# A heads' softmax turned by DMA instead of TensorE, with the value product two pairs later

## The chip, the cores and the metric

The kernel runs on one core of a Trainium2 chip. The metric is the device time of one execution in microseconds (us). The time before the change is 2466.49 us, the median of three runs (2465.38 to 2469.66). The core has TensorE (PE in the profile; its weight loads are listed as PEld), VectorE (DVE), ScalarE (ACT), GpSimd (POOL), and SyncE (SP), whose queue issues most DMA transfers.

## The reference: what is computed

One layer of an encoder on 256 tokens of width 2048, all in float32. Four residual blocks follow one another, each with a layer norm: a SwiGLU network, a mixer of two attention branches, a cross attention to 256 memory tokens, and a second SwiGLU network. The change touches branch A of the mixer: 16 heads of width 64 that look at 64-token chunks, with a clipped relative bias. With 256 tokens and eight previous chunks in view, it is causal by chunk.

```python
def chunked_relbias_attention(q, k, v, rel_bias):
    ...
    scores = jnp.einsum('bcqhd,bckhd->bchqk', qc, kb).astype(jnp.float32) / math.sqrt(d)
    ...
    scores = jnp.where(valid[None, :, None, None, :], scores + bias[None, None], NEG_INF)
    p = jax.nn.softmax(scores, axis=-1).astype(v.dtype)
    o = jnp.einsum('bchqk,bckhd->bcqhd', p, vb)
    return o.reshape(b, s, h * d)

def hybrid_mixer(u, w_in, gate_bias, rel_bias, q_a_norm, w_q_b, kv_a_norm, w_kv_b,
                 w_o_a, w_o_b, w_out, cos, sin):
    ...
    y_a = chunked_relbias_attention(qa.reshape(shp), ka.reshape(shp), va.reshape(shp), rel_bias) @ w_o_a
    y_b = mla_attention(q_lat, kv_lat, q_a_norm, w_q_b, kv_a_norm, w_kv_b, cos, sin) @ w_o_b
    ...
    return (g_a * y_a + g_b * y_b) @ w_out
```

## The kernel before

Weights come in as float32 tiles of 128 x 2048 (1 MB). Each is loaded by a DMA from SP's queue into one of three `raw` buffers, cast by ACT into a `hi` part (fp32r), and the rest is computed by DVE as a `lo` part; there are two buffers each for `hi` and `lo` (`halves`, L245 to L254). Matmuls run over `hi` and `lo` separately (`mm_wide`, L263 and L265): 16 `hi` matmuls of 512 columns, which hold both parts of the activation, and 16 `lo` matmuls of 256.

The program is a list of items, recorded with `add` in the order of the computation, each with the weight tiles that it consumes. `run` walks through it. Before each item it records the loads of the coming weight tiles, as far as two `hi`/`lo` buffers allow, and then the item itself. In the A stage this means that after the first projection of a pair (q) the load of the next pair's first tile is recorded, and after the second (k) that of its second tile. A scheduler then writes out a fixed order for each engine: among the instructions whose inputs are ready by its own reckoning, the one recorded first comes first, with some groups moved ahead by a priority. The softmax has such a priority of 100 instructions. `issue_after` adds an order between two instructions of the same engine without a wait on a result.

Branch A works in eight pairs of heads. For pair i the items are the projections of pair i+1 (`a_proj`, two weight tiles), the turn of pair i−1 (`a_trans`), the scores of pair i with bias and softmax (`a_scores`), and the value product of pair i−1 (`a_out`). Both heads of a pair share the 128 partitions: 64 rows each for the scores, 64 columns each for the value product. The softmax of one head is a 128 x 384 tile: 128 queries by 128 keys, and 128 queries by 256 keys. The value product needs it with keys on partitions. So `a_trans` calls `transpose_p`, which transposes three 128 x 128 blocks of each head on PE (L824) into PSUM and copies them out with ACT (L830). The value product is `pv` (L1027 and L1028). Softmax results and turned tiles are in the `w2` group of working buffers, of which there are six.

During pairs 0 and 1 the latent vectors of branch B are turned as well (`lat_turn`, L927). At the end of A come the rope projections (`rope_items`, weights `w_qr`), whose swap of rows is done by eight small DMAs on SP (L942), and the first heads of B (`b_proj`, weights `w_v` and `w_nope`, and `b_scores`). Two `w2` buffers hold the rope tables then, which POOL loads (L525).

The feed-forward networks do not turn their hidden layer on PE. Their `hidden` copies the float32 words into two planes of 16-bit halves (ACT, L714), sends them through a transposing DMA on SP (L719), and joins the halves again (ACT, L725).

Of the kernel before, what the change touches and what calls it, by code (L numbers as in the profile page):

```python
# [12 lines left out]
U16 = mybir.dt.uint16  # L13
# [5 lines left out]
P = 128  # L19
# [75 lines left out]
class Kernel:  # L95
    def __init__(self, ctx, tc, t, out):
        self.tc, self.nc, self.t, self.out = tc, tc.nc, t, out

        def pool(name, bufs=1, **kw):
            return ctx.enter_context(tc.tile_pool(name=name, bufs=bufs, **kw))  # L100

        self.const = pool("const")
        self.wraw = pool("wraw", 3)
        self.whi = pool("whi", UNITS)
        self.wlo = pool("wlo", UNITS)
        self.blocks = pool("blocks")
        self.res = pool("res")
        self.work = pool("work", 4)
        self.small = pool("small", 4)
        self.ps_mm = pool("ps_mm", 4, space=PSUM)  # L110
        self.ps_at = pool("ps_at", 4, space=PSUM)
        self.items = []
        self.uid = 0
        self.chain = None
        self.cut = False


# [54 lines left out]
    def run(self):  # L172
        queue = [w if isinstance(w, (tuple, Sums)) else (w, None) for _, ws, _, _ in self.items for w in ws]
        ready, nxt, live = [], 0, 0

        def slots(w):
            return 0 if isinstance(w, tuple) and w[1] else 1

        raws, sums = {}, {}

        def fetch(i):
            if i not in raws:
                ap = queue[i].ap if isinstance(queue[i], Sums) else queue[i][0]
                raws[i] = self.raw_tile()
                self.last_load = self.nc.sync.dma_start(raws[i][:, :ap.shape[1]], ap)
            return raws[i]

        def form_sums(i):
            if i < len(queue) and isinstance(queue[i], Sums) and i not in sums:
                raw, home = fetch(i), queue[i].stage  # L190
                sums[i] = self.weight_sums(raw, queue[i].m, self.block(home, (P, 2048)) if home else self.raw_tile())

        def load(i):
            w = queue[i]
            raw = fetch(i)
            form_sums(i)
            if isinstance(w, Sums):
# [12 lines left out]

        def ahead(need, held):
            if nxt < need:
                return True
            n = sum(not early(w) for w in queue[need:nxt])
            return (nxt < need + 5 and (early(queue[nxt]) or n < 2)
                    and held + live + slots(queue[nxt]) <= UNITS)

        done, highs = 0, []
        for fn, ws, held, prio in self.items:
            need = done + len(ws)  # L220
            while nxt < len(queue) and ahead(need, held):
# [471 lines left out]
    def hidden(self, ps, j, g, n, hid, qs):  # L693

        nc = self.nc
        s, u = {}, {}

        def words(v):
            return v.bitcast(U16)

        def product():
            for tt in range(2):
                if qs:
                    up, s[tt] = (qs["add"][tt, a] for a in range(2))
                    nc.vector.tensor_tensor(s[tt], s[tt], ps[tt, 1][:, :n * P], ALU.add)
                    nc.vector.tensor_tensor(up, up, ps[tt, 0][:, :n * P], ALU.add)
                    nc.scalar.activation(s[tt], s[tt], AF.Silu)
                    nc.vector.scalar_tensor_tensor(s[tt], up, 0.5, s[tt], ALU.mult, ALU.mult)
                    u[tt] = up
                else:  # L710
                    s[tt], u[tt] = (self.w2()[:, :n * P] for _ in range(2))
                    nc.scalar.activation(s[tt], ps[tt, 1][:, :n * P], AF.Silu)
                    nc.vector.scalar_tensor_tensor(s[tt], ps[tt, 0][:, :n * P], 0.5, s[tt], ALU.mult, ALU.mult)
                nc.scalar.copy(words(u[tt]).rearrange("p (k c) -> p k c", k=2),  # L714
                               words(s[tt]).rearrange("p (c k) -> p k c", k=2))

        def send():
            for tt in range(2):
                nc.sync.dma_start_transpose(words(s[tt]).rearrange("p (b q) -> p b q", q=P), words(u[tt]))  # L719

        def turn():
            hid.blocks += self.act([f"H{g}"]).blocks
            for tt in range(2):
                with self.tc.issue_after(self.next_hi.ins):
                    nc.scalar.copy(words(u[tt]).rearrange("p (c k) -> p k c", k=2),  # L725
                                   words(s[tt]).rearrange("p (k c) -> p k c", k=2))
# [79 lines left out]
    def softmax(self, s, spans, src=None, scale=1.0):  # L806
        nc = self.nc
        src = s if src is None else src
        n = len(spans)
        m, r = self.sm("sm_m", 2), self.sm("sm_r", 2)  # L810
        for i, (a, b) in enumerate(spans):
            nc.vector.tensor_reduce(m[:, i:i + 1], src[:, a:b], AX.X, ALU.max)
        nc.vector.tensor_scalar(m, m, -scale, None, ALU.mult)
        for i, (a, b) in enumerate(spans):
            nc.scalar.activation(s[:, a:b], src[:, a:b], AF.Exp, bias=m[:, i:i + 1], scale=scale,
                                 accum_out=r[:, i:i + 1])
        nc.vector.reciprocal(r, r)
        for i, (a, b) in enumerate(spans):
            nc.vector.tensor_scalar(s[:, a:b], s[:, a:b], r[:, i:i + 1], None, ALU.mult)

    def transpose_p(self, s, cols, halves=False):
        ps = self.at_tile()
# [11 lines left out]
    def mixer(self, xT, st, steps):  # L834
# [131 lines left out]
        qk, sc, pt = {}, {}, {}  # L966
        oA = {}

        def a_proj(i, side=()):
            def one(k):  # L970
                def fn(w):
                    ps = self.mm_tile()
# [2 lines left out]
                return fn  # L975
            for k in range(2):
                self.add(one(k), t["w_qk"][i, k])
                for f in side[k:k + 1]:
                    self.add(f)

        def scores(parts, spans_q):
# [22 lines left out]
        def a_scores(i):  # L1004
            def fn():
                load_rel(i + 1)
                for j in range(2):
# [4 lines left out]
                    with self.prio(NEAR):  # L1012
                        nc.vector.scalar_tensor_tensor(s[:, :3 * P], ps[:, :3 * P], 1.0 / math.sqrt(A_DIM), bias,
                                                       ALU.mult, ALU.add)
                        self.softmax(s, SPANS)
                    sc[i, j] = s
            self.add(fn)

        def a_trans(i):
            def fn():  # L1020
                for j in range(2):
                    pt[i, j] = self.transpose_p(sc.pop((i, j)), (0, P, 2 * P))
            self.add(fn)

        def pv(ps, v, pT):

# [3 lines left out]
        def a_out(i):  # L1030
            def fn():
# [7 lines left out]
            self.add(fn)  # L1039


        rope_items, rot = [], {}
# [74 lines left out]
            self.add(fn, held=held)  # L1117


        for i in range(NA + 1):  # L1120
            if i + 1 < NA:
                a_proj(i + 1, [lat_turn(i, b) for b in range(2)] if i < 2 else ())
            if i > 0:
                a_trans(i - 1)
            if i < NA:
                a_scores(i)
            if i == NA - 2:
                self.items += rope_items
            if i == NA - 1:
                b_proj(0)  # L1130
                b_proj(1)
            if i > 0:
                a_out(i - 1)
        for h in range(B_HEADS + 1):

            held = int(h % 2 and h + 2 < B_HEADS)
# [6 lines left out]
                b_trans(h - 1, held)  # L1143
            if h + 2 < B_HEADS:
                b_proj(h + 2)
            if h > 0:
                b_out(h - 1, int(h % 2 == 0 and h + 2 < B_HEADS))
            if h in (2, 5, 8, 11):
# [388 lines left out]
```

## Time and profile before

| what | value |
|---|---|
| median of three runs | 2466.49 us |
| profiled execution | 2466.44 us, span 2464.7 us |
| PE busy | 2445.8 us, 99% |
| DVE busy | 2093.3 us, 85% |
| ACT busy | 1447.0 us, 59% |
| granted TensorE clock | 0.998 |
| A pairs in the timeline | scores of pair 0 at 966.6 us, of pair 7 at 1063.5 us |
| `L824` transposes of A and B | 112 instructions, 272 ns median |

The busy time of an engine says how much of the span it works, not whether others wait for it. The chain is followed back from the last instruction to whatever released each step, and so holds what set the time. The timeline lists runs of like instructions with the start of the first; where one row's start is subtracted from the next row's, the result is the time that the run takes up on the engine, which for pipelined matmuls is shorter than the count times the duration.

### The profile page before, as it was taken

The numbers are of one execution on the slowest core, as the hardware profiler recorded it, in microseconds if no ns is written. First come the engines' busy times: TensorE is split into PE (matmuls) and PEld (weight loads), VectorE is DVE, ScalarE is ACT, GpSimd is POOL, SyncE is SP. The second block draws the span as 40 slices with busy tenths as digits, with TensorE's granted clock in tenths as the row PEclk, the third lists the DMA queues.
The fourth block names the chain that finished last, engine by engine and source line by source line (L and its number), as shares of the span: only waits on it lengthen the run. The fifth ranks groups of instructions, "written<-read, shape, count | busy, mean of one in ns | idle before, by whom it ended". The sixth has DMA issues, their size and how long they took to land.

```text
span 2464.7 us, 30068 instructions
## 1 busy us (share of the span) xinstructions
PE 2445.8 (99%) x11603; PEld 2048.8 (83%) x11603; DVE 2093.3 (85%) x2392; ACT 1447.0 (59%) x1932; POOL 37.6 (2%) x81
## 2 busy tenths in 40 slices
PE   9999999999999999999999999999999999999998
PEld 8888888888888888888888888888888888888876
DVE  8999989899778988688788798558879999888886
ACT  6676755676455556556455555545566675557562
POOL 0000000000000001000000000000000000000000
PEclk9999999999999999999999999999999999999999
DMA  7766656666645656554566557544556666666764
GB/s 265 253 217 215 211 203 203 215 197 223 244 156 200 211 205 227 178 174 140 176 235 220 188 179 239 190 161 154 188 197 207 229 221 207 220 213 202 232 210 140
DMA packets 118624, 501.94 MB, mean 204 GB/s; under 512 B 53936, under 2 KB 54704, under 8 KB 63312
## 3 DMA queue, kind: packets, MB, share of 16 engines
q1 hardware_dynamic: 112928, 479.96, 57.4%
q0 software_dynamic: 4688, 18.88, 2.4%
q8 instruction: 91, 1.49, 0.2%
q10 hardware_dynamic: 864, 1.18, 0.1%
q14 instruction: 53, 0.43, 0.1%
HBM read 485.30 MB, written 2.10 MB: 198 GB/s over the span
## 4 chain that ended last, share of the span: by engine, by line
PE 94%; DVE 3%; ACT 1%; DMA 1%; issue 1%; DVEq 0%; SPq 0%; ACTq 0%
PE at L297 24%; PE mm L297 24%; PE at L351 10%; PE mm L351 10%; PE mm L263 9%; PE mm L284 7%; PE mm L265 4%; PE at L986 1%; PE at L284 1%; DVE lo L253 1%; DMA raw<-ffn_w_in_r 1%; PE at L824 1%; PE at L1027 0%; PE at L1346 0%; ACT hi L250 0%
## 5 line engine op out<-in xcount | busy, mean ns | idle before, releaser
L250 ACT CAST hi<-raw 128x1024 fp32r<-128x1024 f32 (+1 forms) x852 | 804.8, 985 | 493.0 <-PE at L297 155.8
L253 DVE TENSOR_TENSOR lo<-raw,hi 128x2048 fp32r<-128x2048 f32 (+1 forms) x427 | 904.7, 2120 | 190.4 <-ACT hi L250 187.7
L297 PE MATMUL mm<-hi,T 128*128 128x512 f32 (+1 forms) x1232 | 288.8, 383 | 0.6 <-ACT hi L250 0.4
L250 ACT CAST X<-H 128x1024 fp32r<-128x1024 f32 (+1 forms) x166 | 170.7, 1034 | 171.3 <-DVE H L235 125.5
L297 PEld LDWEIGHTS mm<-hi,T 128*128 128x128 f32 x1232 | 229.0, 188 | 44.4 <-ACT hi L250 1.1
L297 PE MATMUL at<-hi,T 128*128 128x512 f32 x1072 | 256.7, 389 | 0.0
L253 DVE TENSOR_TENSOR X<-H,X 128x2048 fp32r<-128x2048 f32 (+1 forms) x83 | 186.7, 2250 | 65.0 <-ACT X L250 64.8
L297 PEld LDWEIGHTS at<-hi,T 128*128 128x128 f32 x1072 | 201.1, 188 | 42.0
L297 PE MATMUL mm<-lo,T 128*128 128x512 f32 (+1 forms) x616 | 148.2, 382 | 0.0
L297 PE MATMUL at<-hi,H 128*128 128x512 f32 x592 | 140.8, 390 | 0.0
L297 PE MATMUL at<-lo,T 128*128 128x512 f32 x536 | 132.5, 389 | 0.0
L297 PEld LDWEIGHTS mm<-lo,T 128*128 128x128 f32 x616 | 114.7, 188 | 20.9
L297 PEld LDWEIGHTS at<-hi,H 128*128 128x128 f32 x592 | 110.9, 188 | 23.5 <-DVE w L661 0.6
L263 PE MATMUL mm<-T,hi 128*128 128x512 f32 x512 | 123.7, 393 | 0.0
L297 PEld LDWEIGHTS at<-lo,T 128*128 128x128 f32 x536 | 100.6, 188 | 20.9
L237 DVE TENSOR_TENSOR H<-H,raw 128x512 f32<-128x512 f32 (+1 forms) x166 | 112.3, 676 | 2.3
L263 PEld LDWEIGHTS mm<-T,hi 128*128 128x128 f32 x512 | 93.8, 188 | 19.1 <-issue 0.7
L297 PE MATMUL mm<-hi,H 128*128 128x512 f32 x448 | 108.1, 391 | 0.0
L235 DVE TENSOR_TENSOR H<-raw 128x1024 f32<-128x1024 f32 (+1 forms) x83 | 99.4, 1198 | 4.5 <-DMA raw<-w_gate 4.4
L297 PEld LDWEIGHTS mm<-hi,H 128*128 128x128 f32 x448 | 83.6, 188 | 17.2 <-DVE w L272 0.2
L351 PE MATMUL mm<-X,X 128*128 128x512 f32 x348 | 93.1, 392 | 0.0
L250 ACT CAST X<-raw 128x1024 fp32r<-128x1024 f32 (+1 forms) x54 | 55.3, 1034 | 50.9 <-DVE raw L237 36.9
(331 smaller groups left out, 4074.1 us busy)
## 6 DMA issues: line engine op xcount, KB each, us to landing
raw<-ffn_w_in SPq DMA_DIRECT2D x150, 1024.0 KB, 4.9
raw<-ffn_w_out SPq DMA_DIRECT2D x66, 1024.0 KB, 4.9
raw<-w_gate SPq DMA_DIRECT2D x32, 1024.0 KB, 4.9
raw<-ffn_w_out_r SPq DMA_DIRECT2D x16, 1024.0 KB, 4.9
raw<-w_qk SPq DMA_DIRECT2D x16, 1024.0 KB, 5.0
raw<-w_o_b SPq DMA_DIRECT2D x16, 1024.0 KB, 4.8
raw<-w_out SPq DMA_DIRECT2D x16, 1024.0 KB, 4.9
raw<-w_xk SPq DMA_DIRECT2D x16, 1024.0 KB, 5.1
```

The lines of the kernel that those rows point to most:

```text
L235: self.nc.vector.tensor_tensor(two[0], two[1], raw[:, :m].unsqueeze(1).to_broadcast([P, 2, m]), ALU.add)
L237: self.nc.vector.tensor_tensor(t[:, a * m:a * m + m], t[:, b * m:b * m + m], raw[:, a * m:a * m + m], ALU.add)
L250: self.last_hi = self.nc.scalar.copy(hi[:, c:d], src[:, c:d])
L253: self.nc.vector.tensor_tensor(lo[:, :n], src, hi[:, :n].bitcast(F32), ALU.subtract)
L263: self.nc.tensor.matmul(ps, hi[j], x.both(kt), start=(j == 0), stop=False)
L265: self.last_mm = self.nc.tensor.matmul(ps[:, :S], lo[j], x.at(0, kt), start=False, stop=(j == n - 1))
L284: self.last_mm = self.nc.tensor.matmul(ps, x.at(xi, kt)[:, tt * P:(tt + 1) * P], w[wi][:, j * 512 + c:j * 512 + c + m], start=(start and j ...
L297: self.last_mm = self.nc.tensor.matmul(ps[tt, g][:, :n], x.at(xi, kt)[:, tt * P:(tt + 1) * P], w[wi][:, c:c + n], start=first and j + wi + ...
L351: self.last_mm = self.nc.tensor.matmul(bank[:, :m], a[xi], v[wi][:, c * m:(c + 1) * m], start=own and first and wi + xi == 0, stop=own and ...
L824: self.nc.tensor.transpose(ps[:, i * P:(i + 1) * P], s[:, c:c + P], self.ident)
L986: nc.tensor.matmul(ps[:, c0:c0 + nk], q[:, tt * P:(tt + 1) * P], k[:, :nk], start=(j == 0), stop=(j == len(parts) - 1))
```

## The change

Branch A's softmax results are turned in the way of the hidden layer. `a_scores` now ends with two plane copies (`planes`) into new `w2` tiles. `a_send(i)` issues the two transposing DMAs. `a_join(i)` puts the halves together into the tile that the value product reads. `a_trans` is gone, and branch B keeps `transpose_p`.

The order of the items for pair i becomes: first projection of pair i+1, send of pair i−1, value product of pair i−2, second projection of pair i+1, join of pair i−1, scores of pair i. For the last pair the two rope groups stand in the place of the projections. The join is ordered behind the latest cast recorded (`self.last_hi`), and each weight load recorded after a send is ordered behind that send on SP's queue (`self.sent`). The value products of pairs 6 and 7 move among the first items of branch B. The helpers of the hidden layer are rewritten as methods that both uses share.

```diff
@@ run
+                with self.tc.issue_after(self.sent.ins) if self.sent is not None else nullcontext():
+                    self.last_load = self.nc.sync.dma_start(raws[i][:, :ap.shape[1]], ap)
-                self.last_load = self.nc.sync.dma_start(raws[i][:, :ap.shape[1]], ap)
...
+    def words(self, v, n):
+        return v.bitcast(U16)[:, :2 * n]
+
+    def planes(self, s, u, n):
+        return self.nc.scalar.copy(self.words(u, n).rearrange("p (k c) -> p k c", k=2),
+                                   self.words(s, n).rearrange("p (c k) -> p k c", k=2))
+
+    def send(self, s, u, n):
+        return self.nc.sync.dma_start_transpose(self.words(s, n).rearrange("p (b q) -> p b q", q=P), self.words(u, n))
+
+    def join(self, s, u, n, behind=None):
+        with self.tc.issue_after((behind or self.next_hi).ins):
+            self.nc.scalar.copy(self.words(u, n).rearrange("p (c k) -> p k c", k=2),
+                                self.words(s, n).rearrange("p (k c) -> p k c", k=2))
...
@@ a_scores
                     sc[i, j] = s
+                for j in range(2):
+                    pt[i, j] = self.w2()
+                    self.planes(sc[i, j], pt[i, j], 3 * P)
...
-        def a_trans(i):
+        def a_send(i):
             def fn():
                 for j in range(2):
-                    pt[i, j] = self.transpose_p(sc.pop((i, j)), (0, P, 2 * P))
-            self.add(fn)
+                    self.sent = self.send(sc[i, j], pt[i, j], 3 * P)
+            return fn
+
+        def a_join(i):
+            return lambda: [self.join(sc.pop((i, j)), pt[i, j], 3 * P, self.last_hi) for j in range(2)]
...
-        for i in range(NA + 1):
+        for i in range(NA):
+            side = [lat_turn(i, 0)] if i < 2 else [], [lat_turn(i, 1)] if i < 2 else []
+            if i > 0:
+                side[0].append(a_send(i - 1))
+                side[1].append(a_join(i - 1))
+            if i > 1:
+                side[0].append(a_out(i - 2))
             if i + 1 < NA:
-                a_proj(i + 1, [lat_turn(i, b) for b in range(2)] if i < 2 else ())
-            if i > 0:
-                a_trans(i - 1)
-            if i < NA:
-                a_scores(i)
-            if i == NA - 2:
-                self.items += rope_items
-            if i == NA - 1:
-                b_proj(0)
-                b_proj(1)
-            if i > 0:
-                a_out(i - 1)
+                a_proj(i + 1, side)
+            else:
+                for k in range(2):
+                    self.items += rope_items[2 * k:2 * k + 2]
+                    for f in side[k]:
+                        self.add(f)
+            a_scores(i)
+        b_proj(0)
+        self.add(a_send(NA - 1), held=1)
+        self.add(a_out(NA - 2), held=1)
+        b_proj(1)
+        self.add(a_join(NA - 1))
...
             if h + 2 < B_HEADS:
                 b_proj(h + 2)
+            if h == 1:
+                self.add(a_out(NA - 1))
```

More of the change, by code (lines that the diff above doesn't have):

```diff
@@ L113, in __init__ @@
         self.uid = 0
-        self.chain = None
+        self.chain = self.sent = None
         self.cut = False
@@ L696, in hidden @@
         s, u = {}, {}
-        def words(v):
-            return v.bitcast(U16)
         def product():
@@ L713, in product @@
                     nc.vector.scalar_tensor_tensor(s[tt], ps[tt, 0][:, :n * P], 0.5, s[tt], ALU.mult, ALU.mult)
-                nc.scalar.copy(words(u[tt]).rearrange("p (k c) -> p k c", k=2),
-                               words(s[tt]).rearrange("p (c k) -> p k c", k=2))
+                self.planes(s[tt], u[tt], n * P)
         def send():
             for tt in range(2):
-                nc.sync.dma_start_transpose(words(s[tt]).rearrange("p (b q) -> p b q", q=P), words(u[tt]))
+                self.send(s[tt], u[tt], n * P)
         def turn():
@@ L723, in turn @@
             for tt in range(2):
-                with self.tc.issue_after(self.next_hi.ins):
-                    nc.scalar.copy(words(u[tt]).rearrange("p (c k) -> p k c", k=2),
-                                   words(s[tt]).rearrange("p (k c) -> p k c", k=2))
+                self.join(s[tt], u[tt], n * P)
                 hi, lo = (hid.blk(a, 4 * g, n)[:, :, tt * P:(tt + 1) * P] for a in (0, 1))
@@ L967, in mixer, with a_proj @@
         oA = {}
-        def a_proj(i, side=()):
+        def a_proj(i, side=((), ())):
             def one(k):
@@ L977, in a_proj @@
                 self.add(one(k), t["w_qk"][i, k])
-                for f in side[k:k + 1]:
+                for f in side[k]:
                     self.add(f)
@@ L1038, in fn @@
                 self.split(ps[:, :S], oA["t"].at(0, i), oA["t"].at(1, i))
-            self.add(fn)
+            return fn
         rope_items, rot = [], {}
@@ L1117, in b_out @@
             self.add(fn, held=held)
-        for i in range(NA + 1):
-            if i + 1 < NA:
-                a_proj(i + 1, [lat_turn(i, b) for b in range(2)] if i < 2 else ())
-            if i > 0:
-                a_trans(i - 1)
-            if i < NA:
-                a_scores(i)
-            if i == NA - 2:
-                self.items += rope_items
-            if i == NA - 1:
-                b_proj(0)
-                b_proj(1)
-            if i > 0:
-                a_out(i - 1)
+        for i in range(NA):
[5 more added lines that the diff above has]
+                side[0].append(a_out(i - 2))
+            if i + 1 < NA:
+                a_proj(i + 1, side)
+            else:
+                for k in range(2):
+                    self.items += rope_items[2 * k:2 * k + 2]
+                    for f in side[k]:
+                        self.add(f)
[5 more added lines that the diff above has]
+        self.add(a_join(NA - 1))
         for h in range(B_HEADS + 1):
```

## The prediction

> **What bounds the kernel now.** I read the page first: engine totals and the chain that ended last.
>
> ```profile
> span 2464.7 us, 30068 instructions
> PE 2445.8 (99%) x11603; PEld 2048.8 (83%) x11603; DVE 2093.3 (85%) x2392; ACT 1447.0 (59%) x1932; POOL 37.6 (2%) x81
> PE 94%; DVE 3%; ACT 1%; DMA 1%; issue 1%; DVEq 0%; SPq 0%; ACTq 0%
> ```
>
> TensorE (PE) is busy 99% of the span and holds 94% of the chain, so an instruction that leaves PE shortens the run unless PE then waits. Next the busy time by stretches, for one regular A pair and for the passage from A to B. Columns: stretch, length, busy us (and count) of PE, weight loads, DVE, ACT and POOL, granted clock, DMA share, GB/s.
>
> ```profile
> 995.00:1008.60 13.60, 13.60 (x87) 11.50 (x86) 9.06 (x20) 7.50 (x18) 1.05 (x3) 1.00 0.52 182
> 1049.60:1063.50 13.90, 13.90 (x88) 11.55 (x87) 10.88 (x25) 8.68 (x22) 1.13 (x2) 1.00 0.54 164
> 1063.50:1080.00 16.50, 16.26 (x87) 12.27 (x86) 16.04 (x26) 8.92 (x23) 0.00 (x0) 1.00 0.49 161
> ```
>
> In an A pair PE has no idle time, ACT (ScalarE) is busy 7.50 of 13.60 us, the DMA engines 0.52. In the passage DVE (VectorE) is busy 16.04 of 16.50. Then PE's timeline of one pair.
>
> ```profile
> 994.20 0.82 PE L824 MATMUL at<-ident,w 128*128 128x128 f32 x6
> 994.95 0.93 PE L986 MATMUL at<-w,w 64*128 64x128 f32 x8
> 995.81 0.66 PE L1027 MATMUL at<-w,H 128*64 128x256 f32 x4
> 996.29 0.40 PE L1028 MATMUL at<-w,H 128*64 128x128 f32 x4
> 996.62 3.92 PE L263 MATMUL mm<-T,hi 128*128 128x512 f32 x16
> 1000.38 2.08 PE L265 MATMUL mm<-T,lo 128*128 128x256 f32 x16
> 1002.30 3.82 PE L263 MATMUL mm<-T,hi 128*128 128x512 f32 x16
> 1005.95 2.08 PE L265 MATMUL mm<-T,lo 128*128 128x256 f32 x16
> 1007.86 0.82 PE L824 MATMUL at<-ident,w 128*128 128x128 f32 x6
> ```
>
> From start to start: six transposes 994.95 − 994.20 = 0.75 us, scores 0.86, value product 0.81, first projection 5.68, second 5.56: a period of 13.66 us.
>
> **Removed: the 48 transposes on PE.** 8 pairs x 0.75 = 6.0 us. The last pair costs more, since its product waits for the copy out of PSUM:
>
> ```profile
> 1076.05 0.88 PE L824 MATMUL at<-ident,w 128*128 128x128 f32 x6
> 1077.17 0.65 PE L1027 MATMUL at<-w,H 128*64 128x256 f32 x2 [0.24 <-ACT w L830]
> 1077.74 1.20 PE L263 MATMUL mm<-X,hi 128*128 128x512 f32 x4
> ...
> 1079.33 0.32 PE L1028 MATMUL at<-w,H 128*64 128x128 f32 x1
> ...
> 1080.13 0.73 PE L263 MATMUL mm<-X,hi 128*128 128x512 f32 x2
> ```
>
> 1077.17 − 1076.05 = 1.12 instead of 0.75, so 7 x 0.75 + 1.12 = 6.4 us leave PE. The duration of one transpose would say something else:
>
> ```profile
> L824 PE MATMUL at<-ident,w x112: 270/272/329, 979.9 to 1690.4; 128*128 128x128 f32 x112
> L830 ACT COPY w<-at x32: 454/482/502, 980.5 to 1177.8; 128x384 f32<-128x384 f32 x32
> ```
>
> 272 ns each is latency; six start within 0.75 us, 0.125 each. The Trainium skill, "TensorE: Matmul & The Clock Gate", Part 4, budgets about 275 ns for such a transpose in a kernel. By that the gain would be 48 x 0.275 = 13 us; the trace agrees with the duration and not with its use as a price. ACT also loses 16 copies of 0.48 us (L830), in which PE's next work hid them.
>
> **Added on ACT and SP.** The hidden layer of the FFN already makes this turn, on 128x1024 words and, in its short group, on 128x768, the size of one A head:
>
> ```profile
> L714 ACT COPY w<-w x44: 828/1047/1049, 55.2 to 2356.3; 128x1024 uint16<-128x1024 uint16 x40, 128x768 uint16<-128x768 uint16 x4
> L725 ACT COPY w<-w x44: 1055/1358/1388, 81.9 to 2378.9; 128x1024 uint16<-128x1024 uint16 x40, 128x768 uint16<-128x768 uint16 x4
> L719 SPq DMA_TRANSPOSE w<-w x44: 1211/1232/3807, 56.3 to 2357.7; - x44
> DMA to landing us min/median/max: 3.0/3.5/6.2
> ```
>
> Per head: laying out the planes 0.83 us and joining them 1.06 on ACT, 1.23 on SP to issue, about 3.5 to land. Per pair ACT's load grows by 2 x (0.83 + 1.06) − 2 x 0.48 = 2.8 us: 7.5 becomes 10.3 of a period of 13.66 − 0.75 = 12.91. That is 80%, hidden beside PE's projections. Transfers grow by 2 heads x 128 x 1536 bytes = 0.39 MB a pair, on DMA engines that are half idle. On ACT the joins wait for the landing; behind them stand the planes and the next casts, for which PE waits. The transposes stand ahead of the next load on SP, so I take that wait to be over when the load's cast starts. The Trainium skill, "VectorE: DVE Perf Modes", section "The three transpose paths", speaks against the change: 1309 ns for a 128x128 block of 2-byte values through the DMA. By it a pair's twelve blocks would take an estimated 15.7 us instead of the period of 13.66, 2.0 us a pair slower. The trace disagrees: eight blocks land 3.5 us after issue.
>
> **Moved: weight loads stand behind the sends.** SP works in order. Every load that is recorded after a send must now follow it, and the send waits for the softmax and its planes. Projection weights of a pair's second half (k) are the ones recorded right after a send. The present slack:
>
> ```profile
> 998.67 0.40 ACT L815 ACTIVATE w<-w,sm_m 128x128 f32<-128x128 f32 x1 [1.55 <-DVE sm_m L813]
> 1000.35 0.19 ACT L815 ACTIVATION_READ_ACCUMULATOR w<-w,sm_m 128x1 f32 x1
> 1000.77 0.55 DVE L819 TENSOR_SCALAR w<-w,sm_r 128x128 f32<-128x128 f32 x2
> 1000.63 2.00 ACT L250 CAST hi<-raw 128x1024 fp32r<-128x1024 f32 x2
> 1002.65 2.29 DVE L253 TENSOR_TENSOR lo<-raw,hi 128x2048 fp32r<-128x2048 f32 x1 [1.33 <-ACT hi L250]
> ```
>
> This cast ends at 1002.63. Its matmuls start when the projections, transposes, scores and product that follow are through, at 1007.86 + 0.75 + 0.86 + 0.81 = 1010.28: 7.7 us of slack now. The price of a load behind a send is in the FFN:
>
> ```profile
> 220.96 0.33 SPq L185 DMA_DIRECT2D raw<-ffn_w_in  x1
> DMA to landing us min/median/max: 6.6/6.6/6.6
> 260.62 4.63 SPq L719 DMA_TRANSPOSE w<-w  x2
> 265.34 62.40 SPq L185 DMA_DIRECT2D raw<-ffn_w_out  x13
> DMA to landing us min/median/max: 5.3/5.3/5.3
> ```
>
> 6.6 us is the landing of the load issued at 220.96, between two transposes; 5.3 that of the first load at 265.34, right behind two.
>
> A ring closes: six working buffers hold two softmax results and two turned tiles per pair, so the planes of pair i need the buffers that the joins of pair i−1 free; these joins are recorded behind the cast of the load that stands behind the send of pair i−1, which waits for its planes. One turn, from the last planes on: send 1.23, load issue about 0.1, landing 5.3, cast 2.0, two joins 2.1, two planes 1.7: 12.4 us, against PE's 12.91. With 6.6 it is 13.7. The exponentials (998.67 to 1000.54, 1.9 us) fit into the wait for the landing if ACT's order has them there. So the ring runs just inside PE's period. I take it as hidden, at 0, with 7.7 us of slack to begin with; its ends are in the rivals. If the cover goes, the late thing is the hi cast of the second projection.
>
> **Moved: the value product.** It needs the joins. Counted from the scores at 0, exponentials end no sooner than 4.7 (5.6 in the rows above), the cast follows (2.0) and the joins (1.06 each): the two heads are ready near 7.7 and 8.7. The first projection ends at 0.86 + 5.68 = 6.5. So the product is not ready where it stands, and comes a little later inside the second projection; that alone costs nothing, as PE has the projection to do. But the two heads come ready about 1 us apart, and may be issued apart. Together they take 0.81 us (995.81 to 996.62); apart, in the rows from 1077.17, 0.57 + 0.80 = 1.37. I charge 0.56 for the six pairs in the regular rhythm: 3.4 us. The ends are 0 (both ready) and 7 x 0.56 = 3.9.
>
> **The passage and POOL.** The rope rotation takes two of the same working buffers; POOL's loads of it wait for them today too.
>
> ```profile
> 1049.90 1.17 POOL L525 DMA_DIRECT2D w<-rope x2 [5.91 <-ACT w L830]
> 1057.73 7.98 SPq L942 DMA_DIRECT2D T<-T  x8
> ```
>
> Now they wait for the product of pair 5, some 9 us after the scores of pair 6. The eight rope copies on SP come between sends; the loads of w_nope and w_v follow sends, and B's first heads wait for the last joins' buffers. B's projections can stand in PE's order meanwhile. I put this passage at a loss of 0 to 3 us and take 0, since before the change its DVE work (26.9 of 30.4 us) leaves about the 3 us that PE gives up there (0.80 + 1.12 and a torn product). POOL's bias loads keep their place. The FFN edit only renames its helpers; the wait on an old send in later stages is long satisfied: 0.
>
> **The sum.** −6.4 + 3.4 = −3.0 us against the profiled execution's 2466.44 (1.7 us beyond its span): 2463.5. The median of the runs shown, 2466.49, is the same time.
>
> **Rivals.** First, the full gain: heads joined together in time, nothing torn: 2466.4 − 6.4 = 2460.0. For it: ACT is idle 20% and the landing may be 3.0. Against it: the joins stand behind a late cast.
>
> Second, slower: the ring exceeds PE's period. It decides from a turn of 13.66 us on, that is a landing above 6.5, or exponentials that stand behind the cast in ACT's order. A turn of 13.7 gives nothing back but the torn products: +0.8 x 6 − 3.0 = about +2. With the exponentials in the ring it is 13.7 + 1.9 = 15.6, 2.7 a pair over six pairs, +16 − 3.0 = +13. Half way, +7 or 2473. For it: 6.6 was measured, w1 and the next load follow one another at once, and all margins are below 1 us. Against it: a load behind both sends landed in 5.3, and the first slack is used up before PE waits.
>
> Third, nothing gained: what PE gives up in the stage is taken back in the passage, where DVE is full: +3 to the sum, 2466.5.
>
> Two prices that the rows nearly exclude. The turns themselves as the bound: two heads one after the other at the longest landing, 6.2, take 12.4 us, still inside 12.91. From 6.8 us a head on they would hold PE at the old period; at 7.8, 2.0 us a pair over 8 pairs, the time would be 2482. The page on VectorE named above is the rule for it. And each transpose as 272 ns of PE: 2466.4 − 13.1 = 2453, which the start-to-start times contradict; the page on TensorE is the rule for that.
>
> **Chances and range.** Forecast with torn products 0.40 (2461.6 to 2465.5), full gain 0.27, 272 ns a transpose 0.01, ring too long 0.23 (0.17 of it above 2471.4), nothing gained 0.07, turns as the bound 0.02. A measurement of this kernel can tell about 0.2%, 4.9 us, from no change. Faster (below 2461.5): 0.27 + 0.01, and 0.04 out of the forecast for fewer torn pairs, 0.32. Slower: 0.17 + 0.02, and 0.02 for a passage that loses its 3 us on top of a ring, 0.21. The rest, 0.47, is within. Range 2459.5 to 2474: it leaves out a few of the full gains and the upper third of the long rings.
>
> **What would show it.** PE's timeline of a pair has no L824 and a period of 12.9 to 13.5. L1027 in fours: full gain; in twos: torn. PE idle before the second projection's hi matmuls, released by the cast: the ring. Planes waiting on joins in ACT's rows, SP waiting on planes for most of the period: the ring is near. Landing of w_qk loads beyond 6.5 us, or a period at or above 13.66, would make the prediction wrong; so would PE idle time above 2 us between 1049 and 1080.

## The result, and the profile after

The kernel after takes 2480.16 us (median of six runs, 2478.89 to 2483.05) against 2467.18 for the kernel before in the same comparison (2465.38 to 2469.66): a ratio of 1.0053, 95% interval 1.0042 to 1.0063. It is slower by 13 us, outside the predicted range.

The totals of the page of the kernel after:

```profile
span 2478.1 us, 30009 instructions
PE 2446.6 (99%) x11555; PEld 2045.9 (83%) x11555; DVE 2094.3 (85%) x2392; ACT 1466.4 (59%) x1948; POOL 38.2 (2%) x81
```

PE has 48 instructions fewer, and its busy time has not fallen (2446.6 us, 2445.8 before). The span is 13.4 us longer. So the removed time came back as idle time, and as matmuls that take longer. Where, PE's timeline shows, here from the scores of pair 2 to those of pair 5 in the kernel after (pairs are counted from 0; columns: start, busy time, engine, line, operation, tiles, shapes, count, and in brackets the idle time ahead with what ended it):

```profile
996.32 0.93 PE L996 MATMUL at<-w,w 64*128 64x128 f32 x8
997.19 3.94 PE L264 MATMUL mm<-T,hi 128*128 128x512 f32 x16
...
1004.09 0.65 PE L1043 MATMUL at<-w,H 128*64 128x256 f32 x2 [1.06 <-ACT w L828]
...
1005.00 0.65 PE L1043 MATMUL at<-w,H 128*64 128x256 f32 x2
...
1005.79 3.92 PE L264 MATMUL mm<-T,hi 128*128 128x512 f32 x16
...
1011.56 0.93 PE L996 MATMUL at<-w,w 64*128 64x128 f32 x8
...
1025.18 0.93 PE L996 MATMUL at<-w,w 64*128 64x128 f32 x8
...
1033.60 0.65 PE L1043 MATMUL at<-w,H 128*64 128x256 f32 x2 [1.71 <-ACT w L828]
...
1035.71 5.10 PE L264 MATMUL mm<-T,hi 128*128 128x512 f32 x16
...
1042.66 0.93 PE L996 MATMUL at<-w,w 64*128 64x128 f32 x8
```

The transposes are gone, but the period is 1011.56 − 996.32 = 15.24 us instead of 13.66, and from 1025.18 to 1042.66 even 17.48. PE stands still ahead of the value product until ACT's join (L828) is done, and then the product runs in two halves (L1043 in twos). The projection that follows the longest of these waits took 5.10 us instead of 3.92, at a lower clock (last section). What ACT and SP do in that turn, from the timeline of all engines of the kernel after:

```profile
993.47 1.05 SPq L186 DMA_DIRECT2D raw<-w_qk  x2
...
999.34 2.00 ACT L251 CAST hi<-raw 128x1024 fp32r<-128x1024 f32 x2 [2.53 <-DMA raw<-w_qk]
1001.24 0.40 ACT L810 ACTIVATE w<-w,sm_m 128x128 f32<-128x128 f32 x1
...
1003.01 1.94 ACT L828 COPY w<-w 128x768 uint16<-128x768 uint16 x2
1004.82 1.56 ACT L820 COPY w<-w 128x768 uint16<-128x768 uint16 x2
...
1005.66 2.54 SPq L824 DMA_TRANSPOSE w<-w  x2
...
1008.26 1.05 SPq L186 DMA_DIRECT2D raw<-w_qk  x2
...
1013.80 2.00 ACT L251 CAST hi<-raw 128x1024 fp32r<-128x1024 f32 x2 [1.77 <-DMA raw<-w_qk]
```

One turn reads off as: sends at 1005.66, the load behind them at 1008.26, its landing at 1013.80, the cast there, and then exponentials, joins and planes before the next sends. ACT stood idle for 2.53 us ahead of the cast at 999.34, waiting for the load, and the exponentials (L810) ran only after that cast, at 1001.24. They do not fill the wait; they stand behind it. How fast the turns follow one another is read from the sends. SP's rows of the first and the seventh pair of sends in the kernel after:

```profile
976.54 2.55 SPq L824 DMA_TRANSPOSE w<-w  x2
...
1065.55 2.66 SPq L824 DMA_TRANSPOSE w<-w  x2
```

Six turns take 89.0 us, 14.8 us each.

The places where PE lost time add up to most of the span's difference. Starts of the scores of pair 0, of those of pair 6, and of the last rope part of B's scores, from PE's timelines (one profiled execution each); e1 to e11 are experiments below:

| kernel | pair 0 | pair 6 | last of B | pair 0 to 6 | pair 6 to last of B |
|---|---|---|---|---|---|
| before | 966.58 | 1049.59 | 1171.33 | 83.01 | 121.74 |
| after | 967.35 | 1055.86 | 1183.71 | 88.51 | 127.85 |
| e1, loads not behind sends | 966.01 | 1045.68 | 1171.11 | 79.67 | 125.43 |
| e2, joins not behind the latest cast | 966.35 | 1046.80 | 1177.17 | 80.45 | 130.37 |
| e3, product at the scores | 966.26 | 1050.11 | 1187.68 | 83.85 | 137.57 |
| e4, no turn at all | 966.21 | 1046.15 | 1168.88 | 79.94 | 122.73 |
| e6, e1 with the product at the scores | 968.17 | 1046.88 | 1170.79 | 78.71 | 123.91 |
| e8, e1 with less for DVE | 969.51 | 1049.17 | 1172.60 | 79.66 | 123.43 |
| e9, e6 with less for DVE | 967.19 | 1045.90 | 1169.32 | 78.71 | 123.42 |
| e11, e4 with the product at the scores | 967.18 | 1046.16 | 1168.68 | 78.98 | 122.52 |

After against before: +5.5 us in the regular pairs, +6.1 in the passage to B and in B, and +0.8 ahead of pair 0. The change does not touch what stands ahead of pair 0, and its start differs by up to 3.5 us between these executions (966.01 to 969.51), so the first column says nothing of an edit.

### The profile page after: what moved, and what is told of

It is laid out like the page before. It is cut to its first block, busy times and chain, and to the rows that moved or that the text cites. A ratio compares the mean times of both kernels' runs of the same rounds, so it can differ in the third digit from the quotient of the medians.

```text
span 2478.1 us, 30009 instructions
## 1 busy us (share of the span) xinstructions
PE 2446.6 (99%) x11555; PEld 2045.9 (83%) x11555; DVE 2094.3 (85%) x2392; ACT 1466.4 (59%) x1948; POOL 38.2 (2%) x81
## 4 chain that ended last, share of the span: by engine, by line
PE 52%; DVE 2%; DMA 1%; ACT 1%; issue 0%; DVEq 0%; SPq 0%; ACTq 0%
PE at L298 14%; PE mm L298 12%; PE mm L264 6%; PE mm L285 5%; PE mm L352 5%; PE at L352 5%; PE mm L266 3%; PE at L285 1%; PE at L996 1%; DVE lo L254 1%; PE at L1370 0%; PE at L1346 0%; PE at L1043 0%; PE at L834 0%; DMA raw<-w_xv 0%
```

## The experiments

Theory: the loads that stand behind the sends close a ring over SP, DMA and ACT that is longer than PE's period. Rival: the value product is at fault by its place ahead of the second projection, where it waits for joins that come late anyway.

### e1: the loads are not ordered behind the sends

```diff
-                with self.tc.issue_after(self.sent.ins) if self.sent is not None else nullcontext():
-                    self.last_load = self.nc.sync.dma_start(raws[i][:, :ap.shape[1]], ap)
+                self.last_load = self.nc.sync.dma_start(raws[i][:, :ap.shape[1]], ap)
```

> The changed kernel without the order that puts each weight load behind the last send on SP's queue; everything else is as in it. Theory 'ring': the cast of a pair's second weight tile waits for a load that stands behind the send, the exponentials of the next pair stand behind that cast on ACT, and the planes and the next send behind them; the turn of this ring, about 15 us, sets the pace of the A stage. With loads free the ring is open, the casts wait for no DMA, a pair's period falls to 13 to 13.7 us, and the time to 2464 to 2470. Rival 'place': PE waits because the value product stands ahead of the second projection in its order while the joins come late in any case; then the waits of PE for the joins (5.6 us in the A stage and its end) stay, and the time stays within 2475 to 2480.

Measured: 2466.01 us against 2466.74 before, 0.9995 (0.9986 to 1.0004). PE's timeline of e1:

```profile
992.86 0.93 PE L995 MATMUL at<-w,w 64*128 64x128 f32 x8
...
999.50 0.66 PE L1042 MATMUL at<-w,H 128*64 128x256 f32 x4
...
1006.06 0.93 PE L995 MATMUL at<-w,w 64*128 64x128 f32 x8
...
1076.32 0.79 PE L263 MATMUL mm<-X,hi 128*128 128x512 f32 x1 [4.17 <-DVE w L272]
```

No wait is left in the pair, the product comes whole (in fours), and the period is 1006.06 − 992.86 = 13.20 us. All 13 us of the loss are gone by this one order, with the product at the same place: the ring is the cause. But the kernel is no faster than before: its pairs 0 to 6 take 3.3 us less than before, and the passage, which now holds a wait of 4.17 us, 3.7 us more.

### e2: the joins are not ordered behind the latest cast

```diff
-            return lambda: [self.join(sc.pop((i, j)), pt[i, j], 3 * P, self.last_hi) for j in range(2)]
+            return lambda: [self.join(sc.pop((i, j)), pt[i, j], 3 * P) for j in range(2)]
```

> The changed kernel with the joins ordered behind the cast of the next weight tile to be used, as in the hidden layer, instead of behind the latest cast recorded. Loads still stand behind the sends. 'Ring': the turn loses the step from the late cast to the joins (2 us of cast and the wait for the landing, some 5 us), so the joins come before it and the ring closes only through the planes; the period falls below 14 us and the time to 2466 to 2473. 'Place': the joins come earlier than in the changed kernel, PE's wait for them shrinks from 5.6 us to under 2, and the product of the two heads still comes apart; 2472 to 2477.

Measured: 2471.68 us, 1.0019 (1.0010 to 1.0029). PE's timeline of e2:

```profile
1006.69 0.93 PE L996 MATMUL at<-w,w 64*128 64x128 f32 x8
...
1019.90 0.93 PE L996 MATMUL at<-w,w 64*128 64x128 f32 x8
...
1059.83 2.08 PE L264 MATMUL mm<-X,hi 128*128 128x512 f32 x4 [3.68 <-DVE T L273]
```

The joins may now run while ACT would wait for the load, and so leave the ring. The pairs have periods of 13.2 to 13.7 us, the product comes whole (in fours), and some 8 us of the 13 come back. That agrees with the ring, not with the place of the product. But the ring is not open. The first and the seventh pair of sends in e2:

```profile
975.53 2.55 SPq L824 DMA_TRANSPOSE w<-w  x2
...
1061.26 2.54 SPq L824 DMA_TRANSPOSE w<-w  x2
```

A turn still takes 14.3 us without the joins, as the exponentials and planes still stand behind the cast of the late load. That is more than PE's period, so the pairs live on the slack that the cast of the second projection starts with, and what stays of the loss is in the passage (130.37 us, 8.6 above the kernel before).

### e3: the product behind the joins, directly ahead of the scores

```diff
-                side[0].append(a_out(i - 2))
+                side[1].append(a_out(i - 2))
```

> The changed kernel with the value product of the pair before last recorded behind the second projection and the join, instead of between the two projections. Loads still stand behind the sends. 'Ring': the pace stays that of the ring; PE waits at another place, for the cast of the second tile or for the scores' buffers, and the time stays at 2473 to 2480. 'Place': the product no longer waits and its two heads run side by side, so 5.6 us of waits and about 4.8 us of torn products go: 2468 to 2471.

Measured: 2479.65 us, 1.0051 (1.0036 to 1.0066), as slow as the kernel after. PE's timeline of e3:

```profile
1013.62 3.92 PE L264 MATMUL mm<-T,hi 128*128 128x512 f32 x16 [0.96 <-ACT hi L251]
...
1028.91 5.53 PE L264 MATMUL mm<-T,hi 128*128 128x512 f32 x16 [2.01 <-ACT hi L251]
...
1063.13 0.66 PE L1043 MATMUL at<-w,H 128*64 128x256 f32 x2 [4.40 <-ACT w L828]
```

In the pairs no row of the product waits, and PE now waits for the `hi` cast of the second projection instead, in two of them; in the passage it waits 4.40 us for a join. The place of the product does matter to where the loss falls: pairs 0 to 6 take 83.85 us, 4.7 less than in the kernel after, and from there on it is 137.57, 9.7 more. The pace of the turns is the same:

```profile
975.45 2.55 SPq L824 DMA_TRANSPOSE w<-w  x2
...
1064.70 2.65 SPq L824 DMA_TRANSPOSE w<-w  x2
```

From the first to the seventh pair of sends it is 14.9 us a turn in e3, 14.8 in the kernel after. The place of the product chooses which part of the late ACT work PE meets first, and when; the ring sets how late it is. The rival, by which 2468 to 2471 was expected, is out.

### e4: no turn at all

```diff
-                    pt[i, j] = self.w2()
-                    self.planes(sc[i, j], pt[i, j], 3 * P)
+                    pt[i, j] = sc[i, j]
...
-                for j in range(2):
-                    self.sent = self.send(sc[i, j], pt[i, j], 3 * P)
+                pass
...
-            return lambda: [self.join(sc.pop((i, j)), pt[i, j], 3 * P, self.last_hi) for j in range(2)]
+            return lambda: [sc.pop((i, j)) for j in range(2)]
```

> The order of the changed kernel without any turn: planes, sends and joins of branch A are left out and the value product reads the unturned softmax, so the values are not those of the layer. It measures what leaving the 48 transposes off PE is worth when nothing takes their place. The prediction's 6.4 us: 2460 to 2462, and a period of 12.9 us per pair. If the new order of items has a cost of its own at the passage to branch B, the time stands above that, at 2463 to 2467, and the timeline shows it between the scores of pair 6 and the first scores of B.

Measured: 2463.57 us, 0.9988 (0.9979 to 0.9998). With the turn left out altogether, neither transposes nor their replacement, the gain is 3.2 us and not 6.4. PE's timeline of e4:

```profile
1006.53 0.93 PE L996 MATMUL at<-w,w 64*128 64x128 f32 x8
...
1019.74 0.93 PE L996 MATMUL at<-w,w 64*128 64x128 f32 x8
...
1075.09 1.85 PE L264 MATMUL mm<-X,hi 128*128 128x512 f32 x4 [2.47 <-DVE w L273]
```

The period without any wait is 13.21, where the prediction had 12.91. That is the second of the two cases expected, 2463 to 2467. And a wait of 2.47 us for DVE stands in the passage although nothing there has anything to do with a turn.

### e11 and e12b: what the place of the product costs

Two runs ask why the period is 13.21. Scores use half of the array's rows (64*128 in the rows) and products half of its columns (128*64); in the kernel before they stand side by side, in the kernel after a projection lies between. e11 is e4 with the edit of e3. e12b is the kernel before, with the products of pairs 0 to 4 at their new place and the transposes kept:

```diff
...
             if i + 1 < NA:
-                a_proj(i + 1, [lat_turn(i, b) for b in range(2)] if i < 2 else ())
+                side = [lat_turn(i, 0)] if i < 2 else [], [lat_turn(i, 1)] if i < 2 else []
+                if i > 1:
+                    side[0].append(a_out(i - 2))
+                a_proj(i + 1, side)
...
-            if i > 0:
-                a_out(i - 1)
+            if i >= NA - 2:
+                self.add(a_out(i - 1))
```

> The kernel after, with the planes, the transposing DMAs and the joins left out (the value product reads the softmax results unturned, so a part of the computation is missing), and with the value product recorded behind the second projection, directly ahead of the scores. It differs from the run without a turn by the place of the product alone. Theory of the two array forms (64-row scores and 64-column products cost about 0.2 us more per pair when full-array matmuls stand between them): the period of a pair falls from 13.21 to about 13.0 us, six or seven pairs give 1.2 to 1.5 us, and the run takes 2461.5 to 2463.5. Rival (a period of 13.2 is what the weights or DVE allow, and the product's place is indifferent): the period stays at 13.2 and the time within 2463 to 2464.5.

> The kernel before, with the value products of pairs 0 to 4 moved behind the first projection of the second next pair; the transposes stay on TensorE. Theory of the two array forms: the periods of the pairs whose scores and product stand apart grow from 13.66 to about 13.85 us, with no idle time of PE, and the whole run by about 1 us (2467 to 2469.5). Rival (a change of form costs nothing, the longer periods of the kernel after were waits): the periods stay at 13.66.

Measured: e11 2463.68 us, 0.9987 (0.9977 to 0.9996). e12b 2468.53, 1.0005 (0.9995 to 1.0014), a difference too small to tell by the time alone, but not in PE's timeline, here of e12b:

```profile
997.16 0.93 PE L986 MATMUL at<-w,w 64*128 64x128 f32 x8
...
1001.78 2.07 PE L265 MATMUL mm<-T,lo 128*128 128x256 f32 x16
1003.78 0.66 PE L1027 MATMUL at<-w,H 128*64 128x256 f32 x4
...
1004.59 3.93 PE L263 MATMUL mm<-T,hi 128*128 128x512 f32 x16
1008.35 2.08 PE L265 MATMUL mm<-T,lo 128*128 128x256 f32 x16
1010.26 0.82 PE L824 MATMUL at<-ident,w 128*128 128x128 f32 x6
1011.01 0.93 PE L986 MATMUL at<-w,w 64*128 64x128 f32 x8
```

The period is 1011.01 − 997.16 = 13.85 us, 0.19 above 13.66, with the same matmuls and no idle time. Subtract starts: the `lo` group ahead of the product takes 1003.78 − 1001.78 = 2.00, the one ahead of the transposes 1.91; the `hi` group behind the product takes 3.76, where the kernel before has 3.65 behind a `lo` group. Going into a half-array form costs 0.09 us and coming out of it 0.11. In e11 the product is back at the scores, and its period is 13.02. The Trainium skill, "TensorEngine Tiling (Array Packing)", section "Key Properties", says that a change of tiling mode drains TensorE; the trace agrees in so far as each change costs time here, about 0.1 us each way.

With this the sizes close: 0.75 us of transposes, less 0.09 because a `lo` group now stands ahead of the half-array work, is 0.66 (13.66 − 13.02 = 0.64 measured); less another 0.20 for the second pair of changes, 0.46 (13.66 − 13.21 = 0.45). The rival of e12b, that the longer period was all waits, is out. But e11 was expected at most at 2463.5 and came out no faster than e4. In the profiled executions its pairs won 0.96 us (78.98 us from pair 0 to 6, e4 79.94), and the passage 0.21; its pair 0 began 0.97 later. A gain of about 1 us is less than the medians of these runs can tell (their intervals are about 2.4 us to either side).

### e6, e8, e9 and e10: the passage

These ask for the rest, in the passage, where PE waits for DVE. e6 is e1 with the edit of e3. The other three move one of the two rope multiplications for each group of B's query from DVE to POOL: e8 is e1 with it, e9 is e6 with it, e10 is the kernel before with it.

```diff
-                    nc.vector.tensor_tensor(v, v, rot[g][:, k:k + 1, :].to_broadcast([P, 4, S]), ALU.mult)
+                    (nc.gpsimd if k else nc.vector).tensor_tensor(
+                        v, v, rot[g][:, k:k + 1, :].to_broadcast([P, 4, S]), ALU.mult)
```

> Loads free of the send, and the value product of the pair before last behind the second projection, right ahead of the scores, instead of between the projections. In the run with loads free alone a pair took 13.21 us, not the 12.91 that is left of 13.66 without the transposes: each projection ended 0.09 us later and the first matmuls behind the scores or the product 0.1 us later, once more per pair than before. Theory 'switch': PE pays for each change between the projections' 128-row, 128-column form and the 64-row or 64-column form of the scores and products, so with product and scores together a period is 12.9 us, 0.3 less, and six to seven pairs save 2 us: 2463 to 2465. Rival: the 0.3 us come from DMA transposes or ACT beside PE; then the period stays at 13.2.

> Loads free of the send, and one of the two rope multiplications of each group on POOL instead of DVE. With loads free alone PE stood 4.2 us in the passage to branch B, waiting for DVE, which was never idle there, and ran at a clock of 0.50 for some 5 us after it. Theory 'DVE holds the passage': 2.4 us of DVE work less and the wait shrinks below 2 us, the clock stays up, and the time falls by 3 to 6 us to 2460 to 2463. Rival: the passage is held by the working buffers of the turns (joins of the last pair), not by DVE's load; then the wait stays and the time is 2465 to 2467.

> Both: loads free, product right ahead of the scores, and one rope multiplication of each group on POOL. If switching and DVE in the passage both hold, the gains add: 2458 to 2462, faster than the kernel before. If one of them fails, 2462 to 2466.

> The kernel before with only the rope multiplication moved to POOL, as a control. There PE was idle 0.24 us in the passage, so relieving DVE should give nothing: 2465.5 to 2467.5. If it gives more, what the other runs gain by it is not a matter of the turn.

| kernel | us | before | ratio | 95% interval |
|---|---|---|---|---|
| e6 | 2465.39 | 2467.36 | 0.9992 | 0.9982 to 1.0001 |
| e8 | 2467.16 | 2467.36 | 0.9997 | 0.9988 to 1.0007 |
| e9 | 2463.00 | 2467.36 | 0.9984 | 0.9975 to 0.9994 |
| e10 | 2468.51 | 2467.36 | 1.0005 | 0.9996 to 1.0015 |

e6 has a shorter period (scores at 1007.82 and 1020.84: 13.02, where 12.9 was expected), and its wait in the passage is 3.69 us, for DVE's L272; its time lies just above the 2463 to 2465 expected. e8 has a wait of 2.92, also for L272. In its profile the passage is 2.0 us shorter than in e1 (123.43, 125.43), but the wait did not shrink below the 2 us expected, the clock fell to 0.50 all the same, and the time of 2460 to 2463 did not come. Both together, in e9, on PE's timeline:

```profile
1006.03 0.66 PE L1042 MATMUL at<-w,H 128*64 128x256 f32 x4
...
1006.84 0.93 PE L995 MATMUL at<-w,w 64*128 64x128 f32 x8
...
1071.26 1.89 PE L263 MATMUL mm<-X,hi 128*128 128x512 f32 x4 [2.07 <-ACT X L1092]
1077.01 1.19 PE L263 MATMUL mm<-X,hi 128*128 128x512 f32 x4 [1.14 <-DVE w L272]
```

Product and scores stand together, and the passage still holds 3.2 us of waits. e9 is the version that beats both kernels: the DMA turn with free loads and the late product, and a relieved DVE. It reaches as much as leaving the turn out (e11), and it is 0.16% faster than before, with an interval that leaves no change out; of its two forecasts that is the one in which one theory fails (2462 to 2466). e10, with the DVE edit alone, is not faster: it lies 1 us above the 2465.5 to 2467.5 expected, with a wait of 1.75 us for L272 in its passage that the kernel before does not have. So the gain is not of that edit alone. What in the passage holds back which instruction is not settled: removing 0.2 us per pair (e6, e11), or DVE work (e8), each changed the time by less than these runs can tell, and only the two together (e9) stand clear of the kernel before. DVE, full there, is what most of these waits name; that it is the one cause was not shown.

## Why the prediction was wrong, step by step

**Removed: the 48 transposes on PE (−6.4 us).** Half of it is there. Without any turn the gain is 3.2 us (e4). The count by starts was right for the transposes themselves, 0.75 us a pair. It left out that the transposes, as full-array work ahead of the scores, hid one change of form (0.09 us), and that the passage takes back part of the rest: from pair 6 to the last scores of B, e4 needs 122.73 us against 121.74, with 0.75 + 1.12 = 1.87 us less of transposes in it. This is the third rival, nothing gained, true for about 3 us. That 272 ns is latency and no price held: 13 us were never there to gain.

**Added on ACT and SP (hidden, 0).** Right: e1 has all of it, and no wait in the regular pairs. ACT's work in a pair, by the busy times of the kernel after (columns as in the prediction), is 9.87 us, against an estimate of 10.3:

```profile
1011.60:1025.20 13.60, 13.60 (x83) 11.26 (x82) 8.80 (x18) 9.87 (x19) 1.17 (x3) 1.00 0.61 183
```

**Moved: weight loads behind the sends (a turn of 12.4 us, taken at 0).** This is the step that failed. The prediction had a turn of 12.4 us; the sends came 14.8 us apart. What failed is that "the exponentials (998.67 to 1000.54, 1.9 us) fit into the wait for the landing if ACT's order has them there". From the load at 993.47 to the load at 1008.26 a turn took 14.79 us, and 1.77 of that are exponentials (1001.24 to 1003.01). The other parts, 13.02, came close to 12.4: both sends hold SP for 2.54 us, where one of 1.23 was counted, and the cast began 5.87 us after the issue of its load, not 5.4. ACT's order has the exponentials behind the cast (1001.24 in the rows above), although the maximum for the first exponential was ready two microseconds earlier: the last DVE row of it, in the timeline of the kernel after, is

```profile
998.99 0.16 DVE L808 TENSOR_SCALAR sm_m<-sm_m 128x2 f32<-128x2 f32 x1
```

so it could have begun at 999.15. ACT took its instructions in the written order here, and the exponentials, though ready, ran only when the cast was through. The premise fails on a second count: at 999.15 only 0.19 us of the wait for the load were left, and in the next pair the maximum was ready at 1014.38, after the cast had begun (1013.80). So little of the exponentials could have been hidden in the wait as it was. No run puts them ahead of the cast; what that order would give stays open. The second rival had this case, exponentials in the ring, with a turn of 15.6 us and +13 us; two periods came out at 15.55 and 15.24, and the time at +13. I put the rival at half way between its two prices, and the range ended just above that. That the total agrees is in part luck: the rival took a landing of 6.6 us and counted 2.7 us over each of six pairs, while the turns averaged 14.8, three of the six periods (13.42, 13.62 and 13.20) hardly show the ring, one is 17.48, and half of the loss lies in the passage.

**Moved: the value product (comes later at no cost, torn 3.4 us).** Torn products were there in the kernel after, and at 1.70 us (1004.09 to 1005.79) instead of 0.81 each cost 0.89 and not 0.56; but of the first five products three are torn so and one is whole. They are gone once the ring is (e1, in fours), so they were part of the ring's price and no separate term. "That alone costs nothing, as PE has the projection to do" was wrong: PE too took its instructions in the written order, the product stands ahead of the projection there, and PE waited 5.6 us in five places for the joins:

```profile
ACT hi L251 <- DMA raw<-w_qk: 9.3, 5, 3.2
...
PE at L1043 <- ACT w L828: 5.6, 5, 1.7
```

(The waits of the kernel after from 965 to 1190 us: waiting engine and tile, releaser, then total us, number, longest.) The first row is the root: ACT waits 9.3 us for weights that stand behind sends. The late thing was to be the `hi` cast of the second projection; it is that in e3, where the product does not stand ahead of it. The two changes of form, 0.2 us a pair, also had no term.

**The passage and POOL (0 to 3, taken 0).** The kernel after loses 6.1 us from pair 6 on, outside the bounds given. PE's waits there between 1055 and 1091 come to 6.4 us: 1.39 for a join of the late turn, and 0.42, 0.72, 2.61 and 1.27 for DVE. With free loads (e1) it still loses 3.7.

**The range.** Its upper end cut the slower rival short of its upper price. With two prices for that rival, about 2468 and 2479, decided by a single fact about ACT's order that the trace could not show, both ends belonged inside.

## What to carry to other kernels

Where a DMA is ordered behind another on one queue, follow the chain through every engine that works in order, and put into the turn whatever stands behind the first wait on each of them; work "that fits into the wait" counts as hidden only if the written order has it ahead of the waiting instruction and its inputs are ready in time. Price removed matmuls by starts, together with the changes of array form that they hid. And ask where the freed time can be taken: here the next stretch, with DVE full, took half of it back.

## What the hardware showed

After some idle times of PE the granted clock fell to about half for a few microseconds. The stretches of the kernel after, around the idle time of 1.71 us that ended at 1033.60, and around the one of 2.61 that ended at 1087.15 (columns as in the prediction; the clock is the third number from the end):

```profile
1034.50:1035.70 1.20, 1.19 (x4) 0.60 (x4) 0.00 (x0) 1.20 (x2) 0.00 (x0) 0.63 0.00 0
1035.70:1037.00 1.30, 1.30 (x4) 1.10 (x4) 0.42 (x1) 1.30 (x4) 0.00 (x0) 0.50 1.01 108
1037.00:1038.50 1.50, 1.50 (x5) 1.18 (x5) 0.43 (x1) 1.30 (x3) 0.00 (x0) 0.59 0.38 49
1038.50:1040.50 2.00, 2.00 (x11) 1.62 (x10) 2.00 (x2) 0.00 (x0) 0.00 (x0) 1.00 1.05 164
...
1087.10:1090.00 2.90, 1.65 (x8) 1.28 (x8) 2.90 (x5) 1.42 (x3) 0.00 (x0) 1.00 0.75 138
```

The shorter idle time was followed by 0.50 to 0.63 for 4 us, the longer one by 1.00. In e1 a clock of 0.50 followed the 4.17 us, and in e11 the 2.45 us:

```profile
1073.50:1075.40 1.90, 1.90 (x5) 1.52 (x6) 1.90 (x1) 0.00 (x0) 0.00 (x0) 0.50 0.00 0
```

(A stretch of e11.) After the 1.71 us such a wait so cost an estimated 1.5 to 2 us more than its own length: half of the 3.5 to 4 us at about half the clock. In the kernel after the torn product and the projection that followed took 1.2 + 4.94 us, where they take 0.79 + 3.76 at a clock of 1.00, 1.6 us more. The Trainium skill, "TensorE: Matmul & The Clock Gate", section "What's actually happening", has the clock fall after an idle window of about 3.4 us, with windows that run free of the kernel. The falls after 1.71 and 2.45 us are below that figure, so here the measurement decides. The length of the idle time alone does not decide either: the clock also fell after 2.01 us in e3 and 2.07 in e9, and stayed at 1.00 after 2.33 in e3, 2.40 in e2 and the 2.61. That fits a window whose position matters, but no run separates that from what the array did just before.

The second thing not expected is the price of a change between the full array and half of it: 0.09 us into the half-array form and 0.11 out of it, seen alone in e12b.
